# Placing 56 modulation tiles in another way in a one-core diffusion-layer kernel, with a new order of the first attention head and another split of the second half-step's norm

## The chip, the cores and the metric

The kernel runs on one core of one Trainium2 chip. The time is that of the whole program on the device, in microseconds (us). A core has a matrix engine (TensorE, PE in the profile, with its weight loads listed apart as PEld), a vector engine (VectorE, DVE), a scalar engine (ScalarE, ACT), GpSimd (POOL) and a sequencer that mostly issues DMAs (SyncE, SP). [...]

## The reference, cut to what matters

One layer of a diffusion trunk on 512 latent and 128 context tokens, 1024 channels wide: a half-step of a gated feed-forward network, token mixing (differential attention beside a bidirectional chunkwise mLSTM), and a second half-step. Nine modulation vectors per token kind scale, shift and gate the three stages:

```python
def adaln(cvec, w, b):
    m = jax.nn.silu(cvec) @ w + b          # w_ada: 1024 x 9*1024
    return m.reshape(cvec.shape[0], N_MOD, D_MODEL)

def layer(x, mods, l, p, ctx):
    m = [mods[:, j][:, None, :] for j in range(N_MOD)]
    g = p['g_norm'][l]
    hh = rmsnorm(x, g[0]) * (1 + m[1]) + m[0]
    x = x + 0.5 * m[2] * swiglu(hh, p['ffn1_w1'][l], p['ffn1_w3'][l], p['ffn1_w2'][l])
    hh = rmsnorm(x, g[1]) * (1 + m[4]) + m[3]
    y, ctx_out = token_mixer(hh, p, l, ctx)
    x = x + m[5] * y
    hh = rmsnorm(x, g[2]) * (1 + m[7]) + m[6]
    x = x + 0.5 * m[8] * swiglu(hh, p['ffn2_w1'][l], p['ffn2_w3'][l], p['ffn2_w2'][l])
    return x, ctx_out
```

The modulation is computed twice, with `c` for the latent tokens and with `c_ctx` for the context tokens. In the mixer the attention has 8 heads of two 64-wide query and key halves (each normed, and rotated by position), whose two softmaxes are subtracted; the mLSTM has 4 heads and walks over chunks of 128 tokens in both directions. The two branches go through `w_br_d` and `w_br_m`, are gated, added, and projected by `w_out`.

## The kernel before, in words

**Arithmetic.** Everything is fp32. For TensorE each operand is split into a high part in a shorter format and a low remainder, and a product is three matmuls: high by high, high by low, low by high (`mm3`). A split of a weight is a copy on ScalarE (`wH`, `ww`, `wB`) and a subtraction on VectorE (`wL`). The 640 token columns are worked on in two halves of 320.

**Stages, in order.** (1) Startup and the first two modulation vectors, on TensorE. (2) The first half-step's up products: 18 steps of `products`. (3) Its down products: three groups of the hidden width (`PLAIN_GROUPS`), four steps each, of which eight (20 to 27) call `modulation`. (4) The second norm, the first queries' and keys' projection in token groups (`tok_group` with `w_q`, then `w_k`). (5) Eight attention heads, one loop, with five query blocks `qi` each; between the steps `fill` hands out units of the projections that come later (values, gates, mLSTM queries and keys), so that TensorE has work beside the softmax. (6) Four mLSTM heads of ten chunk cells each (`Memory`), again with `fill` units between the cells. (7) The branch projections `w_brd` and `w_brm`, eight granules of four columns' products, then `w_out` and the third norm (`normed`). (8) The second half-step, which ends with the output.

**The modulation tiles.** 56 tiles of 128 channels remain after the startup, each for one of seven modulation vectors. `Columns` hands them out in order. `place(n, csil, load, ahead)` sets how many come next, from which conditioning rows (`csil`, silu of `c` and of `c_ctx`, spread over all partitions), how a raw tile of `w_ada` is loaded, and how many loads run ahead. `tile` runs two `tensor_tensor_reduce` passes over 128 x 1024 on VectorE, one for each token kind, and then fetches the next. When the eight tiles of a vector are done, its bias is added, and a callback makes what the later stages use: vector 0 (numbered among these seven) gives the first half-step's gate, 1 and 2 the second norm's shift and scale, 3 the mixer's gate, 4 and 5 the third norm's, 6 the last gate.

**Where they stand.** `modulation(i, at)` is called in each of the first half-step's steps, twice (`at` 0 and 1). In steps 2 to 17 it runs one tile for `at` 1, and one more for `at` 0 where `i % 8 == 4`: 18 tiles. In the down products' steps 20 to 27 it runs one tile for `at` 0 and two for `at` 1: 24 tiles. Their raw tiles, rows and scratch lie in the buffers tagged `BL`, `BH` and `CH`, which the last down group's weights (`wB`) use as well. The last 14 stand in the attention loop, in heads 0 to 5; their raw tiles take buffers of the ring `raw` (two buffers), through which all projection weights pass, and their rows lie in `q3` and `k3`, which the fourth pair of queries and keys takes later.

**Head 0.** `Head.pack` copies a head's queries (`qpk`) and keys (`kpk`, `kp2`) into split parts; `queries` and `keys` turn them on TensorE. For head 0 `pack` and `queries` stand in the setup behind both token groups, where `qk_norm_rope` has normed and rotated the queries and then the keys on VectorE.

**The third norm.** `normed` takes one half of the columns. Half 1 consists of 192 latent and 128 context columns (`SEGS`), which have modulation vectors of their own, so each of its eight channel blocks takes two segments of three instructions: scale and divide by the norm on VectorE (`x<-x,scale,ry`), add the shift on ScalarE into the high part `hm`, and subtract on VectorE for the low part. `x` itself is left without its shift; sixteen `activate` instructions (eight blocks by two segments) add it behind the first products, before `operand_sums` adds up blocks of `x` for the second half-step's operands (`S`).

## Time and profile before

Three runs took 1905.3, 1905.95 and 1911.75 us (median 1905.95). The profiled execution has a span of 1909.6 us from its first to its last instruction, that is 3.65 us above the median and within the runs. Its mean granted TensorE clock is 0.982 of full speed.

The stages, each as a stretch of the profiled span (busy time in us; the borders are rounded):

| stretch, us | stage | PE busy | DVE busy | ACT busy | granted clock |
|---|---|---|---|---|---|
| 0 to 60 | startup, first norm | 39.48 | 44.84 | 33.34 | 0.94 |
| 60 to 320 | up products, half-step 1 | 254.15 | 223.70 | 130.39 | 1.00 |
| 320 to 500 | down products, half-step 1 | 167.81 | 126.42 | 35.10 | 0.96 |
| 500 to 575 | second norm, first queries and keys | 64.83 | 57.47 | 38.74 | 0.93 |
| 575 to 1126 | attention heads | 538.14 | 340.07 | 244.45 | 0.99 |
| 1126 to 1290 | mLSTM cells | 158.71 | 98.20 | 95.57 | 0.98 |
| 1290 to 1411 | branch projections | 120.32 | 57.81 | 46.96 | 1.00 |
| 1411 to 1500 | `w_out`, third norm | 88.75 | 63.02 | 47.96 | 1.00 |
| 1500 to 1909 | half-step 2 | 390.34 | 294.62 | 171.73 | 0.98 |

How to read what follows. A line of the timeline has the start, the duration, the engine, the source line, the operation, and what it writes (left of the arrow) and reads; in brackets stands how long its engine had been idle before it, and whose end released it. A line of the groups has busy time and mean duration in ns, then the idle time before and its main releaser. The granted clock is the share of full speed that the chip gave TensorE. The source lines of small helpers (L39, L42, L52, L55) are shared by many operations, so the names of the tiles tell which one it is.

### The profile page before, as it was taken

Reading aid. Unit: us, or ns where it says so; the run is one execution under the profiler, and the core shown is the slowest. Engines: PE = TensorE matmul, PEld = TensorE weight load, DVE = VectorE, ACT = ScalarE, POOL = GpSimd, SP = SyncE. Lnnn points to the kernel's source line nnn. Section 1 sums busy time; section 2 is a strip of 40 time slices with the busy share of each in tenths; the row PEclk is TensorE's granted clock in tenths of the full one; section 3 lists DMA queues with packets and bytes.
Section 4 is the critical chain, followed back from the end, with each engine's and each line's share of the span. In section 5 each row is a group of like instructions: output and inputs, shape, how many; then the busy total and the mean of one; then the engine's idle time right before and its main releaser. Section 6 shows DMA issues by size and latency. Waiting matters only on the chain.

```text
span 1909.6 us, 30786 instructions
## 1 busy us (share of the span) xinstructions
PE 1822.5 (95%) x12658; PEld 1782.0 (93%) x12658; DVE 1306.1 (68%) x2209; ACT 844.2 (44%) x1447; POOL 42.4 (2%) x69
## 2 busy tenths in 40 slices
PE   6999999998989999999999989999999899999989
PEld 4999999998888999999999989899999899999989
DVE  7889986578686566775765536664457778886575
ACT  5644443212353353453544446655234655554232
POOL 1000001010000000000000000000000000000000
PEclk9999999998999999999999999999999899999999
DMA  8354558965314223223221342445442344447952
GB/s 322 117 180 166 174 182 303 339 218 168 139 45 163 98 75 120 79 92 104 70 102 60 107 165 93 141 149 211 163 141 83 127 144 176 174 174 268 346 188 94
DMA packets 127150, 298.77 MB, mean 156 GB/s; under 512 B 9441, under 2 KB 90593, under 8 KB 114337
## 3 DMA queue, kind: packets, MB, share of 16 engines
q1 hardware_dynamic: 115762, 248.58, 37.4%
q0 software_dynamic: 11248, 48.24, 7.0%
q8 instruction: 99, 1.62, 0.4%
q14 instruction: 41, 0.34, 0.1%
HBM read 233.15 MB, written 63.63 MB: 155 GB/s over the span
## 4 chain that ended last, share of the span: by engine, by line
PE 78%; DVE 9%; DMA 8%; issue 3%; ACT 2%; SPq 0%; POOL 0%; DVEq 0%; ACTq 0%; POOLq 0%
PE ps_f L52 35%; PE ps_p L52 21%; PE ps_t L52 11%; PE ps_o L52 2%; PE sc L52 2%; DMA ada<-in_w_ada_c 2%; PE ps_n L52 2%; DVE ww L39 1%; PE ps_wT L55 1%; DMA ada<-csil_dram 1%; PE ps_u L52 1%; PE ps_qkT L55 1%; DMA raw<-in_w2a 1%; DVE ada L671 1%; DVE junk L671 1%
## 5 line engine op out<-in xcount | busy, mean ns | idle before, releaser
L52 PE MATMUL ps_f<-S,ww 128*128 128x320 f32 x1992 | 321.3, 310 | 14.2 <-ACT ww L267 6.9
L52 PEld LDWEIGHTS ps_f<-S,ww 128*128 128x128 f32 x1992 | 299.9, 189 | 16.7 <-DVE ww L39 9.5
L52 PE MATMUL ps_p<-hH,wH 128*128 128x320 f32 x864 | 275.3, 319 | 3.1 <-ACT aT L1313 2.5
L52 PE MATMUL ps_p<-hH,wL 128*128 128x320 f32 x864 | 268.2, 310 | 0.0
L52 PE MATMUL ps_p<-hL,wH 128*128 128x320 f32 x864 | 268.2, 310 | 0.0
L52 PE MATMUL ps_f<-hm,ww 128*128 128x320 f32 x1248 | 198.7, 311 | 9.8 <-ACT ww L267 5.6
L52 PEld LDWEIGHTS ps_f<-hm,ww 128*128 128x128 f32 x1248 | 188.2, 190 | 11.1 <-ACT ww L267 5.9
L52 PE MATMUL ps_t<-wH,hH 128*128 128x256 f32 x640 | 186.6, 292 | 0.9 <-DVE x L42 0.9
L52 PE MATMUL ps_t<-wH,hL 128*128 128x256 f32 x640 | 182.7, 285 | 0.0
L52 PE MATMUL ps_t<-wL,hH 128*128 128x256 f32 x640 | 182.3, 285 | 0.0
L39 DVE TENSOR_TENSOR ww<-raw,ww 128x2048 fp32r<-128x2048 f32 (+1 forms) x62 | 138.7, 2237 | 51.9 <-ACT ww L267 29.7
L52 PEld LDWEIGHTS ps_p<-hH,wH 128*128 128x128 f32 x864 | 163.8, 190 | 4.3 <-ACT aT L1313 2.7
L52 PEld LDWEIGHTS ps_p<-hL,wH 128*128 128x128 f32 x864 | 163.8, 190 | 0.5
L52 PEld LDWEIGHTS ps_p<-hH,wL 128*128 128x128 f32 x864 | 163.4, 189 | 0.0
L52 PE MATMUL ps_f<-hm,wB 128*128 128x320 f32 x1008 | 161.5, 309 | 0.0
L52 PEld LDWEIGHTS ps_f<-hm,wB 128*128 128x128 f32 x1008 | 151.3, 188 | 0.0
L39 DVE TENSOR_TENSOR wL<-raw,wH 128x2048 fp32r<-128x2048 f32 x49 | 112.1, 2288 | 38.1 <-ACT wH L123 37.9
L123 ACT ACTIVATE wH<-raw 128x2048 fp32r<-128x2048 f32 x49 | 93.6, 1911 | 99.0 <-PE ps_p L52 89.5
L52 PEld LDWEIGHTS ps_t<-wH,hH 128*128 128x128 f32 x640 | 124.1, 194 | 1.9 <-ACT hH L201 1.7
L39 DVE TENSOR_TENSOR raw<-raw 128x1024 f32<-128x1024 f32 (+1 forms) x144 | 124.1, 865 | 1.7
L267 ACT ACTIVATE ww<-raw 128x2048 fp32r<-128x2048 f32 x48 | 91.7, 1911 | 74.7 <-PE ps_f L52 47.3
L52 PEld LDWEIGHTS ps_t<-wH,hL 128*128 128x128 f32 x640 | 123.9, 194 | 0.5 <-DVE hL L42 0.5
(294 smaller groups left out, 3251.5 us busy)
## 6 DMA issues: line engine op xcount, KB each, us to landing
g_dram<-g SPq DMA_DIRECT2D x44, 640.0 KB, 5.0
ada<-in_w_ada_c POOLq DMA_DIRECT2D x24, 512.0 KB, 4.9
raw<-in_w1b SPq DMA_DIRECT2D x11, 1024.0 KB, 4.8
raw<-in_w3b SPq DMA_DIRECT2D x11, 1024.0 KB, 4.8
raw<-in_w1a SPq DMA_DIRECT2D x10, 1024.0 KB, 4.8
raw<-in_w3a SPq DMA_DIRECT2D x10, 1024.0 KB, 7.0
hm<-g_dram POOLq DMA_DIRECT2D x8, 1280.0 KB, 10.2
raw_a<-in_w_ada_c POOLq DMA_DIRECT2D x18, 512.0 KB, 5.3
```

The costliest lines, as they stand in the source:

```text
L39: return eng.tensor_tensor(out=out, in0=in0, in1=in1, op=op)
L52: tc.keep_in_program_order(nc.tensor.matmul(*args, **kw))
L55: tc.keep_in_program_order(nc.tensor.transpose(*args, **kw))
L123: act(h, raw, AF.Copy)
L267: act(t[0], flat, AF.Copy)
L671: vec.tensor_tensor_reduce(out=junk, in0=raw, in1=self.csil[:, v, :], op0=ALU.mult, op1=ALU.add, scale=1.0, scalar=0.0, accum_out=mod[:, c ...
```

## The change

- The up products take 8 tiles (in even steps, `at` 1) instead of 18, the down products 16 (one for each call) instead of 24.
- The attention takes 9, in the blocks 0 to 2 of heads 1 to 3, instead of 14. Their raw tile and scratch lie in the buffers `q2` and `k2`, no longer in the ring.
- The remaining 23 stand behind the attention: ten in the mLSTM cells, two in the last mLSTM head's end, the others between the units of the branch projections. They load through the ring again. Their conditioning rows are loaded anew, 1 MB on SP's queue, into a pool of their own that is opened at the attention's end. A load is issued only where `fetch` says so, two units or cells ahead of its tile.
- Head 0's queries are packed directly behind the queries' token group, and its keys later, behind `queries`. Its square scratch (`sq`) lies in the buffer of `qT`.
- The third norm divides by the norm for a block's whole half at once, adds scale and shift by ScalarE in place, segment by segment, copies the high part whole on ScalarE and subtracts whole on VectorE. `x` then holds its shift, and the sixteen later `activate` instructions go.

```diff
-        def fetch(self):
-            while len(self.next) < min(self.ahead, self.n):
+        def fetch(self, ahead=0):
+            while len(self.next) < min(ahead or self.ahead, self.n):
...
-        columns.place(18, csil, load_columns)
+        columns.place(8, csil, load_columns)
...
-                if 2 <= i < 18 and (at or i % 8 == 4):
+                if 2 <= i < 18 and at and i % 2 == 0:
                     columns.tile(hs.at_vec)
...
-                    columns.place(24, csil, load_columns)
+                    columns.place(16, csil, load_columns)
                 columns.tile(hs.at_vec)
-                if at:
-                    columns.tile(hs.at_vec)
...
-        sq = ap.tile([128, 5, 256], F32, tag="pk", name="sq", bufs=2)
+        if pr:
+            sq = ap.tile([128, 5, 256], F32, tag="pk", name="sq", bufs=2)
+        else:
+            sq = ap.tile([128, 5, 256], F32, tag="qT", name="sq")
...
         def pack(self):
-
+            self.pack_q()
+            self.pack_k()
...
             self.turn_features(self.qpk, self.qT, False, lambda o, i: act(o, i, AF.Copy))
+            if self.hd:
+                self.low_keys()
...
     tok_group(psum, [(w_q, i, e_q) for i in (2, 3, 4)], lambda k: None)
+    heads = [Head(hd) for hd in range(8)]
+    heads[0].pack_q()
     tok_group(psum, [(w_k, i, e_k) for i in (2, 3, 4)], lambda k: None)
...
-        heads[0].pack()
         heads[0].queries()
+        heads[0].pack_k()
+        heads[0].low_keys()
...
     def load_columns(src):
-        t = rawp.tile([128, 2048], F32, tag="raw", name="raw_a")
-        dma(t[:, :D], src)
-        return t[:, :D], t[:, D : D + D // 2].bitcast(BF16)
+        t = pair("q", 2, "raw_a").rearrange("p a t -> p (a t)")[:, :D]
+        junk = pair("k", 2, "junk").rearrange("p a t -> p (a t)")[:, : D // 2].bitcast(BF16)
+        dma(t, src)
+        return t, junk
...
-    columns.place(14, csil, load_columns, 1)
+    columns.place(9, csil, load_columns, 1)
...
-            if hd < 6 and qi in (1, 3) or (hd, qi) in ((2, 2), (4, 2)):
+            if hd in (1, 2, 3) and qi < 3:
                 columns.tile()
...
+    cs = ExitStack()
+    cs_p = cs.enter_context(tc.tile_pool(name="csil", bufs=1, side="right"))
+    csil = cs_p.tile([128, 2, D], F32, name="csil")
+    for v in range(2):
+        nc.sync.dma_start(out=csil[:, v, :], in_=csil_dram[v].partition_broadcast(128))
...
+    columns.place(23, csil, load_columns, 0)
...
             fill.slot(0)
+            if len(box_ml) % 4 == 0:
+                columns.fetch(1)
+            elif len(box_ml) % 4 == 2:
+                columns.tile()
+            box_ml.append(0)
         m.stats()
...
         mem[3].finish(i)
+        columns.fetch((i + 1) % 2)
+        if i % 2:
+            columns.tile()
...
+    def drain_beside_columns():
+        n = 0
+        while fill.q:
+            columns.fetch((n + 1) % 2)
+            fill.one()
+            if n % 2 and columns.n:
+                columns.tile()
+            n += 1
...
+            xs = x[d][:, half(hf)]
+            h, lo = hs.hh(d, hf)
+            tt(vec, xs, xs, rs, ALU.mult)
             for s0, s1, j in SEGS[hf]:
-                xs = x[d][:, s0:s1]
-                h, lo = (t[:, s0 - c0 : s1 - c0] for t in hs.hh(d, hf))
-                sh = shift[:, d, j : j + 1]
-                stt(xs, xs, scale[:, 2, d, j : j + 1], rs[:, s0 - c0 : s1 - c0], ALU.mult, ALU.mult)
-                act(h, xs, AF.Identity, bias=sh)
-                ins = stt(lo, xs, sh, h.bitcast(F32), ALU.add, ALU.subtract)
+                v = x[d][:, s0:s1]
+                act(v, v, AF.Identity, bias=shift[:, d, j : j + 1], scale=scale[:, 2, d, j : j + 1])
+            act(h, xs, AF.Copy)
+            ins = tt(vec, lo, xs, h.bitcast(F32), ALU.subtract)
...
-    for d in range(KT):
-        for s0, s1, j in ((0, NS, 0), (NS, T, 1)):
-            xs = x[d][:, s0:s1]
-            act(xs, xs, AF.Identity, bias=m_of(6)[:, d, j : j + 1])
     summed = hs.operand_sums(lambda r: x_pairs[r])
```

More of the change, by code (lines that the diff above doesn't have):

```diff
@@ L1125, in gate_cols, with qk_norm_rope @@
             )
-    def qk_norm_rope(raw, tab):
+    def qk_norm_rope(raw, tab, pr):
         A, B, g = tab
-        sq = ap.tile([128, 5, 256], F32, tag="pk", name="sq", bufs=2)
+        if pr:
+            sq = ap.tile([128, 5, 256], F32, tag="pk", name="sq", bufs=2)
+        else:
+            sq = ap.tile([128, 5, 256], F32, tag="qT", name="sq")
         act(sq, raw, AF.Square)
@@ L1158, in evac @@
                 if i == 4:
-                    qk_norm_rope(t, tabs[0])
+                    qk_norm_rope(t, tabs[0], pr)
             return evac
@@ L1171, in evac @@
                 if i == 4:
-                    qk_norm_rope(t, tabs[1])
+                    qk_norm_rope(t, tabs[1], pr)
                     nc.sync.dma_start(out=a["new_k"][:, pr * 256 : (pr + 1) * 256], in_=t[:, 4, :])
@@ L1199, in pack, with pack_q @@
         def pack(self):
+            self.pack_q()
+            self.pack_k()
+        def pack_q(self):
             hs = slice(self.h * 128, (self.h + 1) * 128)
             qv = q_tok[self.pr][:, :, hs].rearrange("p t (c d) -> p t c d", c=2)
-            kv = self.kv = k_tok[self.pr][:, :, hs].rearrange("p t (c d) -> p t c d", c=2)
             self.qpk = ap.tile([128, 5, 4, 64], F32R, tag="pk", name="qpk", bufs=2)
@@ L1206, in pack, with pack_k @@
             tt(vec, self.qpk[:, :, 1:3, :], qv, self.qpk[:, :, 0::3, :].bitcast(F32), ALU.subtract)
+        def pack_k(self):
+            hs = slice(self.h * 128, (self.h + 1) * 128)
+            kv = self.kv = k_tok[self.pr][:, :, hs].rearrange("p t (c d) -> p t c d", c=2)
             self.kpk = ap.tile([128, 5, 4, 64], F32R, tag="pk", name="kpk", bufs=2)
@@ L1226, in queries, with low_keys @@
             self.turn_features(self.qpk, self.qT, False, lambda o, i: act(o, i, AF.Copy))
+            if self.hd:
+                self.low_keys()
+            ck = load(ap, [128, 2, 256], a["cache_kd"][:, self.hd], tag="asq", name="ck")
+            act(self.kH[:, :, 512:768], ck, AF.Copy)
+            tt(vec, self.kL[:, :, 512:768], ck, self.kH[:, :, 512:768].bitcast(F32), ALU.subtract)
+        def low_keys(self):
             self.kp2 = ap.tile([128, 5, 4, 64], F32R, tag="pk", name="kp2", bufs=2)
@@ L1229, in queries @@
                 self.at_vec = tt(vec, self.kp2[:, :, i::2, :], self.kv, self.kpk[:, :, i::2, :].bitcast(F32), ALU.subtract)
-            ck = load(ap, [128, 2, 256], a["cache_kd"][:, self.hd], tag="asq", name="ck")
-            act(self.kH[:, :, 512:768], ck, AF.Copy)
-            tt(vec, self.kL[:, :, 512:768], ck, self.kH[:, :, 512:768].bitcast(F32), ALU.subtract)
         def keys(self, part):
@@ L1383, in gate_evac @@
         return f
-    heads = [Head(hd) for hd in range(8)]
     with tc.tile_pool(name="gates", bufs=1) as gt:
@@ L1518, in tile_trunk, with load_columns @@
     att.close()
+    cs = ExitStack()
[3 more added lines that the diff above has]
+        nc.sync.dma_start(out=csil[:, v, :], in_=csil_dram[v].partition_broadcast(128))
+    def load_columns(src):
+        t = rawp.tile([128, 2048], F32, tag="raw", name="raw_a")
+        dma(t[:, :D], src)
+        return t[:, :D], t[:, D : D + D // 2].bitcast(BF16)
+    columns.place(23, csil, load_columns, 0)
     ml = ExitStack()
@@ L1668, in attended @@
         aHL.append(split_part(attended.raw[:, k % 3], t))
+    box_ml = []
     mem = [Memory(h) for h in range(4)]
@@ L1731, in tile_trunk @@
         tt(vec, zL[:, k], raw[:, k % 3], zH[:, k].bitcast(F32), ALU.subtract)
-    fill.drain()
+    def drain_beside_columns():
[6 more added lines that the diff above has]
+            n += 1
+    drain_beside_columns()
     ml.close()
@@ L1760, in tile_trunk @@
             nc.sync.dma_start(out=x_pairs[g], in_=x_dram[:, 2 * g : 2 * g + 2, :])
-        fill.drain()
+        drain_beside_columns()
+    cs.close()
     fp = out.enter_context(tc.tile_pool(name="out", bufs=1))
@@ L1805, in normed @@
         rs = st[hf].rstd(psum)
-        c0 = hf * HALF
         shift = m_of(6)
         for d in range(KT):
+            xs = x[d][:, half(hf)]
+            h, lo = hs.hh(d, hf)
+            tt(vec, xs, xs, rs, ALU.mult)
             for s0, s1, j in SEGS[hf]:
-                xs = x[d][:, s0:s1]
-                h, lo = (t[:, s0 - c0 : s1 - c0] for t in hs.hh(d, hf))
-                sh = shift[:, d, j : j + 1]
-                stt(xs, xs, scale[:, 2, d, j : j + 1], rs[:, s0 - c0 : s1 - c0], ALU.mult, ALU.mult)
-                act(h, xs, AF.Identity, bias=sh)
-                ins = stt(lo, xs, sh, h.bitcast(F32), ALU.add, ALU.subtract)
+                v = x[d][:, s0:s1]
+                act(v, v, AF.Identity, bias=shift[:, d, j : j + 1], scale=scale[:, 2, d, j : j + 1])
+            act(h, xs, AF.Copy)
+            ins = tt(vec, lo, xs, h.bitcast(F32), ALU.subtract)
         return ins.ins
```

## The prediction

> **What bounds the kernel now.** I read the engine shares first, then the chain that ended last, then the span in stretches of 20 us, and last the stalls of TensorE one by one in its timeline.
>
> ```profile
> span 1909.6 us, 30786 instructions
> PE 1822.5 (95%) x12658; PEld 1782.0 (93%) x12658; DVE 1306.1 (68%) x2209; ACT 844.2 (44%) x1447; POOL 42.4 (2%) x69
> PE 78%; DVE 9%; DMA 8%; issue 3%; ACT 2%; SPq 0%; POOL 0%; DVEq 0%; ACTq 0%; POOLq 0%
> ...
> 60.00:80.00 20.00, 20.00 (x140) 20.00 (x139) 17.81 (x28) 15.42 (x24) 0.00 (x0) 1.00 0.23 81
> 440.00:460.00 20.00, 14.17 (x97) 13.91 (x95) 17.79 (x33) 1.57 (x3) 2.65 (x5) 0.91 0.54 176
> 460.00:480.00 20.00, 16.96 (x93) 16.57 (x94) 13.92 (x22) 8.18 (x10) 0.00 (x0) 0.75 0.49 170
> 600.00:620.00 20.00, 19.07 (x117) 18.89 (x118) 13.40 (x17) 9.22 (x14) 0.00 (x0) 0.84 0.56 206
> ```
>
> TensorE is busy for all but 87 us of the span and carries 78% of the chain. No matmul is added or taken away, so the change can win only what TensorE idles, plus what it loses at a lower granted clock after idling. The columns of the stretches are length, busy time and count of PE, PEld, DVE, ACT, POOL, then granted clock. An undisturbed stretch holds 140 matmuls, 0.143 us each; the two from 440 to 480 hold 97 and 93, at clocks 0.91 and 0.75. These are TensorE's stalls that the change can touch, with what released it in brackets:
>
> ```profile
> 136.77 1.73 PE L52 MATMUL ps_f<-S,ww 128*128 128x320 f32 x10 [2.56 <-DVE ww L39]
> 239.06 1.15 PE L52 MATMUL ps_f<-S,ww 128*128 128x320 f32 x6 [2.57 <-DVE ww L39]
> 462.16 0.90 PE L52 MATMUL ps_f<-S,wB 128*128 128x320 f32 x2 [7.99 <-ACT wB L285]
> 555.63 1.50 PE L55 MATMUL ps_qkT<-identr,qpk 128*128 128x128 f32 x10 [5.93 <-DVE qpk L39]
> 600.93 1.51 PE L55 MATMUL ps_wT<-ident,p 128*128 128x128 f32 x6 [4.33 <-DVE p L42]
> 742.16 0.87 PE L55 MATMUL ps_wT<-ident,p 128*128 128x128 f32 x6 [1.66 <-DVE p L42]
> 879.22 1.03 PE L55 MATMUL ps_wT<-ident,p 128*128 128x128 f32 x5 [1.91 <-DVE p L42]
> 1515.73 0.90 PE L52 MATMUL ps_f<-S,ww 128*128 128x320 f32 x2 [6.91 <-ACT ww L267]
> 1518.05 2.24 PE L52 MATMUL ps_f<-S,ww 128*128 128x320 f32 x7 [1.42 <-DVE ww L39]
> ```
>
> **The change part by part.** A modulation tile is two passes on VectorE, one DMA of 512 KB, and nothing on TensorE:
>
> ```profile
> L671 DVE CUSTOM_DVE_ANT_0 ada<-ada 128x1024 bf16<-128x1024 f32 x48 | 58.6, 1221 | 17.8 <-DMA ada<-in_w_ada_c 12.0 <-DMA ada<-csil_dram 5.5
> L671 DVE DVE_READ_ACCUMULATOR2_ANT mod<- 128x1 f32 x112 | 9.3, 83 | 0.0
> ```
>
> So a tile costs about 2 x 1.22 = 2.45 us of VectorE; the accumulator reads overlap nearly all of their 0.083 us.
>
> *Up products, 18 tiles to 8.* The stalls at 136.77 and 239.06 wait for a weight's low part on VectorE, which is full there. They fall where the old rule puts two tiles into one step (steps 4 and 12, `i % 8 == 4`). The new rule puts one there: 2.45 us less VectorE ahead of a wait of 2.56. Gain 5.1 (bounds 0 and 5.1). Ten loads leave POOL's queue, where nothing waits for them.
>
> *Down products, 24 tiles to 16.* The conditioning rows and raw tiles lie in the buffers tagged B and C that the last down group's weights need:
>
> ```profile
> 351.97 1.23 DVE L671 CUSTOM_DVE_ANT_0 ada<-ada 128x1024 bf16<-128x1024 f32 x1 [5.46 <-DMA ada<-csil_dram]
> 461.05 1.06 ACT L285 ACTIVATE wB<-raw 128x1024 fp32r<-128x1024 f32 x1 [2.22 <-DVE mod L671]
> 461.52 1.22 DVE L671 CUSTOM_DVE_ANT_0 ada<-ada 128x1024 bf16<-128x1024 f32 x1
> ```
>
> ScalarE's split of `wB` waits for the tiles, and the last pass starts at 461.52. The second of the 48 passes gets its rows at 351.97; from there on the 24 tiles take some 4.6 us each (110 us by 24), their loads waiting for the two raw buffers. Sixteen at that pace end near 352 + 16 x 4.6 = 426, before TensorE has got to the step that the last one is tied to (about 438). `wB` can then be split some 10 us before TensorE wants it at 454. The two stretches lack 280 - 190 = 90 matmuls: gain 90 x 0.143 = 12.9 us, taken as 12.7 (bounds 6, if the 6 us of other stalls there stay, and 12.9).
>
> *Head 0's queries first.* At 555.63 TensorE waits for `qpk`:
>
> ```profile
> 545.05 1.22 DVE L39 TENSOR_TENSOR q_tok<-q_tok,sw 128x1024 f32<-128x1024 f32 x1
> 552.35 0.72 ACT L1205 ACTIVATE qpk<-q_tok 128x640 fp32r<-128x640 f32 x1
> 577.57 1.74 DVE L1262 TENSOR_REDUCE mx<-sc 128x2 f32<-128x1536 f32 x1
> ```
>
> The queries are ready at 546.3, but their packing stands behind the keys' rope and starts at 552.35. Moved ahead of the keys it ends near 548, while TensorE is still busy (until 549.7). So 5.93 us of idle go, with some 1.6 us of half clock. But what is late next is VectorE: keys' rope, `kp2`, the gates' scans, then head 0's first softmax, whose `mx` runs at 577.57 although its scores are there 3 us earlier. That row of work starts only about 1 us sooner, while TensorE comes 6 us sooner and must wait for the score bank. Bounds: 1.0 (VectorE decides) and 7.5 (the softmax slips in between). I take 4.5. `sq` moves to the buffer of `qT`, which is empty then: nothing.
>
> *Nine tiles in heads 1 to 3, in buffers of their own.* The old ones go through the weights' raw ring, and VectorE stands still in front of them:
>
> ```profile
> 594.61 1.22 DVE L671 CUSTOM_DVE_ANT_0 raw_a<-raw_a,csil 128x1024 bf16<-128x1024 f32 x1 [6.25 <-DMA csil<-csil_dram]
> 877.00 1.23 DVE L671 CUSTOM_DVE_ANT_0 raw_a<-raw_a,csil 128x1024 bf16<-128x1024 f32 x1 [1.51 <-DMA raw_a<-in_w_ada_c]
> ```
>
> The tile at 594.61 waits 6.25 us for its rows, and head 0's softmax, whose `p` TensorE awaits at 600.93, stands behind it. Head 0 has no tile any more: 4.33 us go, and with them the low clock that follows (0.84 over 20 us is 3.2; 2.8 of it on busy time): 7.1. The stalls at 742 and 879 have a tile, waiting for its DMA, ahead of `p`. A load now starts when the tile before is done, some 13 us ahead, so its two passes start without a wait and no longer hold `p` up. Gain 1.66 + 1.91 = 3.6. Bounds together 5 and 11.
>
> *Second half-step's norm.*
>
> ```profile
> 1475.83 4.57 DVE L42 SCALAR_TENSOR_TENSOR x<-x,scale,ry 128x192 f32<-128x192 f32 x15
> 1476.28 4.93 ACT L1814 ACTIVATE hm<-x,mod 128x192 fp32r<-128x192 f32 x15 [2.07 <-DVE x L42]
> 1489.05 0.83 DVE L39 TENSOR_TENSOR x<-x 128x640 f32<-128x640 f32 x1 [1.61 <-ACT x L1846]
> 1490.86 1.56 DVE L39 TENSOR_TENSOR x<-x 128x640 f32<-128x640 f32 x2 [0.99 <-ACT x L1846]
> L1846 ACT ACTIVATE x<-x,mod 128x512 f32<-128x512 f32 x8 | 5.7, 716 | 0.0
> L39 DVE TENSOR_TENSOR nacc<-nacc,nsq 128x320 f32<-128x320 f32 x36 | 17.6, 490 | 16.4 <-ACT nsq L181 15.0
> ```
>
> VectorE's second half falls from 32 pieces at 0.305 us (4.57 by 15), 9.8 us, to 16 whole ones at 0.49 or less, 7.8 at most. ScalarE gets eight copies there (about 0.45 each: 3.6) and drops the shifts behind (16, of which the eight long ones are 5.7 us). The norm is now paced by ScalarE, about 8 x (2 x 0.33 + 0.4) = 8.5 us, so it ends near 1485 as before. What goes is the wait of the operand sums for the shifts, 1.61 + 0.99 = 2.6 us, and sums can start in VectorE's gaps before 1485. From 1491 VectorE works without a pause up to the weights that TensorE awaits at 1515.73 and 1518.05 (8.3 us idle). Gain 5 (bounds 1.5 and 9, the latter with the clock that follows).
>
> *23 tiles behind the attention.* New here: two loads of the conditioning rows (1 MB) on SP's queue, then ten tiles in the mLSTM cells and 13 in the projections, loaded through the raw ring.
>
> ```profile
> 1137.34 0.83 DVE L39 TENSOR_TENSOR P<-P,mask 128x640 f32<-128x640 f32 x1 [7.69 <-DMA P<-nm_dram]
> 1137.61 0.71 PE L52 MATMUL ps_st<-mqT,mkT 128*128 128x128 f32 x4 [1.42 <-ACT stage L1381]
> 1240.00:1260.00 20.00, 20.00 (x123) 18.36 (x121) 14.88 (x48) 12.27 (x36) 0.00 (x0) 1.00 0.50 160
> DVE C L42 <- PE ps_u L52: 23.3, 15, 4.0
> L39 DVE TENSOR_TENSOR wL<-raw,wH 128x2048 fp32r<-128x2048 f32 x49 | 112.1, 2288 | 38.1 <-ACT wH L123 37.9
> raw_a<-in_w_ada_c SPq DMA_DIRECT2D x14, 512.0 KB, 3.9
> raw<-in_w_brm SPq DMA_DIRECT2D x4, 1024.0 KB, 6.9
> 1339.73 1.92 ACT L123 ACTIVATE wH<-raw 128x2048 fp32r<-128x2048 f32 x1 [12.22 <-PE ps_p L52]
> ```
>
> The rows are issued ahead of `va` and `P`, for which VectorE and ScalarE already stand still and TensorE begins to wait at 1136. In head 0 VectorE stood 6.25 us for the same rows (above). I price the delay at 4.5 (bounds 0 and 7). In the cells VectorE is busy 15 of 20 us and waits 23.3 us for TensorE in all; a pass of 1.22 us can hold up an update of `C`, for which the next cell but one has about 2 us of slack: ten tiles, 0.3 us each, 3 (bounds 0 and 24.5). In the projections ScalarE waits 12.22 us with the next weight already there, so the ring has slack: 1 for the 13 (bounds 0 and 40, below).
>
> **Sum:** -5.1 - 12.7 - 4.5 - 7.1 - 3.6 - 5.0 + 4.5 + 3 + 1 = -29.5. The span of 1909.6 becomes 1880; it is 3.65 above the median of 1905.95, and lies within the runs (1905.3 to 1911.75), so I forecast 1905.95 - 29.5 = **1876 us**.
>
> [...]
>
> **Rivals.** (1) *The cells pay for the tiles*: each of the ten exposes one pass or more (1.22 to 2.45) and the rows cost 7. That is 12 to 24 instead of 3 and 2.5 more: 1888 to 1900. For it: VectorE is in order and the cells are a recurrence; against it: its 5 idle us in 20. (2) *Head 0 and the last norm give nothing*, as VectorE's row of work decides both: 1.0 + 1.5 for 9.5: 1883. (3) *The change doesn't free the last down group*: `wB` then waits for its own weight's DMA or for a tile tied late; 6 us less: 1882. (4) *Slower: the ring starves the projections.* It has two buffers, and a weight (load 6.9, split 1.9 + 2.3) and two tiles (3.9 + 2.45 each) must pass in the 14.1 us of a granule. Were they to follow each other on one buffer, 11.1 + 12.7 = 23.8 us a granule, 9.7 more, eight times: 1954. It outweighs the rest from 29.5 / 8 = 3.7 us per granule. Against it: the two buffers offer 28 us for 24.
>
> **How the numbers follow.** Forecast (1868 to 1884) 0.55; rival 2 or 3 alone 0.15 (within or close to it); both, or rival 1: 0.20; rival 4: 0.05; better than 1868 0.05. The best bounds together give -45, the worst of the gains with the dear cells about -10. The range is 1861 to 1895. A measurement of this kernel can tell about 0.5% (9.5 us) from no change: faster 0.83, same 0.10, slower 0.07.
>
> **What would show it.** Right: no stall over 1 us near 137, 239, 462, 600, 742 and 879; the stretches 440 to 480 at 138 to 140 matmuls each; the first score bank as the next stall behind 550; under 5 us idle ahead of the second half-step's first sums. Wrong: `PE <- DVE C` or `num` in the cells, ACT `wH` waiting for DMA in the projections, or `wB` still behind `mod`.

## The result, and the profile after

The changed kernel takes 1893.48 us (median of four runs, 1888.11 to 1896.81), the kernel before 1905.62 us beside it: a ratio of 0.9924 with a 95% interval of 0.9902 to 0.9947. In later runs it was 1894.09 and 0.9934 (0.9918 to 0.9951). So it is faster by 12 to 13 us, and not by the 29.5 that lead to the forecast of 1876. The time lies in the range of 1861 to 1895, near its upper end.

The page of the changed kernel begins like this (span, engine shares, chain of waits by engine):

```profile
span 1890.2 us, 30782 instructions
PE 1816.4 (96%) x12658; PEld 1778.2 (94%) x12658; DVE 1299.5 (69%) x2193; ACT 847.0 (45%) x1447; POOL 32.9 (2%) x51
PE 79%; DVE 9%; DMA 7%; ACT 3%; issue 2%; SPq 0%; DVEq 0%; ACTq 0%
```

The matmuls are the same 12658; TensorE's idle time in the span fell from 87 us to 74. The stretches that answer to those shown of before, and one more (length, busy time and count of PE, PEld, DVE, ACT, POOL, granted clock, DMA share, GB/s):

```profile
440.00:460.00 20.00, 20.00 (x138) 20.00 (x137) 9.87 (x18) 5.58 (x9) 0.00 (x0) 1.00 0.23 79
460.00:480.00 20.00, 19.14 (x129) 18.59 (x128) 14.60 (x35) 7.11 (x14) 0.00 (x0) 1.00 0.20 68
600.00:620.00 20.00, 18.49 (x141) 18.20 (x140) 16.02 (x31) 6.98 (x16) 0.00 (x0) 1.00 0.39 132
1320.00:1340.00 20.00, 15.33 (x90) 15.10 (x89) 12.54 (x19) 3.82 (x2) 0.00 (x0) 0.83 0.78 290
```

From 440 to 480 the row now has 138 and 129 matmuls instead of 97 and 93 (the second stretch already holds the next stage's beginning). The last row shows a new loss: the changed kernel has 90 matmuls from 1320 to 1340, where before had 138:

```profile
1320.00:1340.00 20.00, 20.00 (x138) 20.00 (x138) 6.60 (x12) 3.74 (x5) 0.00 (x0) 1.00 0.37 137
```

TensorE's stalls in the changed kernel's timeline show the same:

```profile
348.82 3.02 PE L52 MATMUL ps_f<-hm,ww 128*128 128x320 f32 x10 [2.14 <-DVE ww L39]
536.09 1.28 PE L55 MATMUL ps_qkT<-identr,kpk 128*128 128x128 f32 x10 [1.72 <-ACT kpk L1216]
562.53 0.87 PE L55 MATMUL ps_wT<-ident,p 128*128 128x128 f32 x6 [3.25 <-DVE p L42]
636.88 0.87 PE L55 MATMUL ps_wT<-ident,p 128*128 128x128 f32 x6 [1.73 <-DVE p L42]
1111.88 1.20 PE L52 MATMUL ps_n<-va,P 128*128 128x258 f32 x2 [4.60 <-DVE P L39]
1333.87 0.60 PE L52 MATMUL ps_p<-hH,wH 128*128 128x320 f32 x1 [4.67 <-DVE y L39]
1495.49 0.71 PE L52 MATMUL ps_f<-S,ww 128*128 128x320 f32 x2 [2.74 <-ACT ww L267]
1497.82 2.50 PE L52 MATMUL ps_f<-S,ww 128*128 128x320 f32 x8 [1.62 <-DVE ww L39]
```

The stalls at 137, 239, 462, 601, 742 and 879 are gone. New ones stand at 562.53 and 636.88, ahead of `p`, and, longer, at 1111.88 and 1333.87. To see what each stage won or lost, take a product that both kernels have at its border, and subtract its start. Here are the borders in the timeline of before (the second norm, the attention's end, a product in the first and one in the last mLSTM cells, the third norm), and then the same products in that of the changed kernel:

```profile
506.07 0.81 PE L52 MATMUL ps_ss<-nacc,ones 128*128 128x320 f32 x2 [3.45 <-DVE nacc L39]
1126.67 0.41 PE L52 MATMUL ps_p<-hH,wH 128*128 128x320 f32 x1 [2.47 <-ACT aT L1313]
1156.41 0.60 PE L52 MATMUL ps_n<-va,P 128*128 128x258 f32 x2
1287.97 0.60 PE L52 MATMUL ps_n<-va,P 128*128 128x258 f32 x2
1470.10 0.70 PE L52 MATMUL ps_ss<-nacc,ones 128*128 128x320 f32 x2
```

```profile
484.83 0.91 PE L52 MATMUL ps_ss<-nacc,ones 128*128 128x320 f32 x2 [3.46 <-DVE nacc L39]
1095.12 0.41 PE L52 MATMUL ps_p<-hH,wH 128*128 128x320 f32 x1 [2.47 <-ACT aT L1324]
1127.31 0.59 PE L52 MATMUL ps_n<-va,P 128*128 128x258 f32 x2
1261.84 0.59 PE L52 MATMUL ps_n<-va,P 128*128 128x258 f32 x2
1451.62 0.70 PE L52 MATMUL ps_ss<-nacc,ones 128*128 128x320 f32 x2
```

The lag is -21.24 at the second norm, -31.55 at the attention's end, -29.10 in the first mLSTM cells, -26.13 in the last, -18.48 at the third norm and -19.4 at the end of the span. Its steps, beside the forecast's terms and the same sums for a second profile of the changed kernel (after_again, whose span is 1892.1):

| stage | forecast, us | changed kernel | after_again |
|---|---|---|---|
| startup and half-step 1 | -17.8 | -21.2 | -19.3 |
| head 0 and attention | -15.2 | -10.3 | -8.2 |
| conditioning rows, first cells | +4.5 | +2.5 | +1.1 |
| other cells | +3.0 | +3.0 | +2.1 |
| projections | +1.0 | +7.7 | +7.6 |
| third norm, half-step 2 | -5.0 | -0.9 | -0.8 |
| sum | -29.5 | -19.4 | -17.5 |

### The profile page after: what moved, and what is told of

It is laid out like the page before. It is cut to its first block, busy times and chain, and to the rows that moved or that the text cites. A ratio compares the mean times of both kernels' runs of the same rounds, so it can differ in the third digit from the quotient of the medians.

```text
span 1890.2 us, 30782 instructions
## 1 busy us (share of the span) xinstructions
PE 1816.4 (96%) x12658; PEld 1778.2 (94%) x12658; DVE 1299.5 (69%) x2193; ACT 847.0 (45%) x1447; POOL 32.9 (2%) x51
## 4 chain that ended last, share of the span: by engine, by line
PE 79%; DVE 9%; DMA 7%; ACT 3%; issue 2%; SPq 0%; DVEq 0%; ACTq 0%
PE ps_f L52 41%; PE ps_p L52 17%; PE ps_t L52 11%; DMA raw_a<-in_w_ada_c 3%; PE sc L52 2%; PE ps_o L52 2%; DMA ada<-csil_dram 1%; PE ps_n L52 1%; DVE junk L671 1%; PE ps_wT L55 1%; DMA P<-nm_dram 1%; PE ps_qkT L55 1%; DVE raw_a L671 1%; PE ps_u L52 1%; DVE wL L39 1%
## 5 line engine op out<-in xcount | busy, mean ns | idle before, releaser
L52 PEld LDWEIGHTS ps_f<-hm,ww 128*128 128x128 f32 x1248 | 190.4, 192 | 10.3 <-ACT ww L267 5.9
L52 PEld LDWEIGHTS ps_t<-wL,hH 128*128 128x128 f32 x640 | 123.7, 193 | 0.3 <-issue 0.2
```

The lines of the kernel that those rows point to most:

```text
L52: tc.keep_in_program_order(nc.tensor.matmul(*args, **kw))
```

## The experiments

All times stand beside runs of the kernel before on the same chip. The spread of one kernel's runs is some 5 to 10 us, so a difference under 3 us is read from the traces, not from the times.

### The two kernels again

before_again is the kernel before, after_again the changed kernel, both without an edit.

> The kernel before, unchanged, to see what differs between two profiled executions of one kernel. The profiled execution of before took 1911.75 us, 6 us above the other three (1905.3 to 1906). Theory A: it held a stall that the usual execution has not (first candidate: the 6.25 us for the conditioning rows in head 0, whose removal I priced at 7.1); then this profile has a span near 1903.5, and one or two of the stalls at 137, 239, 359, 462, 556, 601, 742, 879 are missing or over 2 us shorter. Theory B: the 6 us lie spread over many places, all those stalls are there within 0.5 us, and the forecast's terms stand. Ratio to before 1.000 within 0.002.

Measured: 1908.38 us, ratio 1.0009 (0.9995 to 1.0023), span 1908.9. The profile has all those stalls: 2.56, 2.55, 2.27, 6.37, 5.92, 3.62, 1.58 and 1.96 us where the first had 2.56, 2.57, 2.70, 7.99, 5.93, 4.33, 1.66 and 1.91. Theory B holds in the main: all the stalls are there, though not within its 0.5 us. They differ by up to 0.7, the one of 7.99 by 1.6. The trace on which the forecast rests is no odd one, though both profiled executions of before (1911.75 and 1910.65 us) are longer than the medians beside them by 2 to 6 us.

> The changed kernel again, more rounds. If the first profile was an ordinary execution: span 1890 to 1893, a ratio to before of 0.990 to 0.992. If it was a good one: ratio 0.992 to 0.994, and the new profile shows where executions differ. Own_ym3 against this run is 6 to 10 us if the projections' 7.7 us are what it wins.

Measured: 1894.09 us, ratio 0.9934, span 1892.1. The span fits the first case of the expectation and the ratio the second, so the first profile was at most some 2 us better than an ordinary one. The two traces of the changed kernel differ by 2 us in half-step 1 and by 2 us in the attention, with the same large stalls in the same places.

### The hand-over from w_brd to w_brm

A drain is the loop that runs the units still left in `fill`, with a tile behind every second one: the first drain ends the `w_brd` products, the second does the `w_brm` products. Between the two a new PSUM pool is opened. What happened there, before the stall at 1333.87, is seen on SP, ScalarE and VectorE of the changed kernel:

```profile
1305.46 16.50 SPq L74 DMA_DIRECT2D raw_a<-in_w_ada_c  x4
1324.32 3.96 SPq L74 DMA_DIRECT2D raw<-in_w_brm  x2
1329.09 1.91 ACT L123 ACTIVATE wH<-raw 128x2048 fp32r<-128x2048 f32 x1 [17.93 <-PE ps_p L52]
1331.03 2.29 DVE L39 TENSOR_TENSOR wL<-raw,wH 128x2048 fp32r<-128x2048 f32 x1 [2.31 <-ACT wH L123]
1333.24 0.48 DVE L39 TENSOR_TENSOR y<-ps_p,sig 128x320 f32<-128x320 f32 x1
```

Four tiles' loads occupy the ring for 16.5 us; the first `w_brm` weight, which the program has behind them, is issued at 1324.32 and split by 1333.3. In before it was issued at 1320.98, more than 30 us ahead of its use. The stall is put down to `y`, and rightly: the `y` at 1333.24 is the last of sixteen, and with it the last evacuation of the old PSUM pool. TensorE's last `w_brd` product had ended at 1329.2, but this `y` stands on VectorE behind `wL`, the split of the late weight, for which VectorE idles 2.31 us until `wH` is done. So the late weight holds TensorE up by way of the last `y`.

brm_early queues the weight ahead of the last two tiles (the first drain ends when four granules are left):

```diff
+    for g in range(4):
+        fill.granule(a["w_brm"][g], lambda g=g: feat_units(psum, m_evac(g), zHL))
-    drain_beside_columns()
+    drain_beside_columns(4)
```

> The changed kernel with the four w_brm granules queued ahead of the first drain, so that the first of their weights is loaded ahead of the drain's last two tiles. Theory: the 7.7 us lost between 1300 and 1340 come from the raw ring; the four tiles of the first drain hold both buffers, and the first w_brm weight is issued only at 1324.3, split until 1333. Then the stall of 4.67 us (released at 1333.87) and the low clock behind it go: 5 to 8 us faster than the changed kernel (about 1886 to 1888.5; ratio to before 0.989 to 0.991). Rival: VectorE's own work (ten passes of 1.22 us among the evacuations) makes the loss; then the stall stays or moves, and the time is within 2 us of the changed kernel's 1893.5.

Measured: 1892.24 us, ratio 0.9924. The weight was split by 1325.9, and the stall stayed:

```profile
1329.59 1.23 DVE L671 CUSTOM_DVE_ANT_0 raw_a<-raw_a,csil 128x1024 bf16<-128x1024 f32 x1 [1.00 <-DMA raw_a<-in_w_ada_c]
1332.29 0.48 DVE L39 TENSOR_TENSOR y<-ps_p,sig 128x320 f32<-128x320 f32 x1
1332.92 0.61 PE L52 MATMUL ps_p<-hH,wH 128*128 128x320 f32 x1 [5.63 <-DVE y L39]
```

The rival came true in a narrower form. The next product needs a bank of the new PSUM pool, so it waits for the last `y`; here this `y` stood on VectorE behind a tile that had waited for its load, and no longer behind `wL`.

tail_clear leaves no tile to the last `w_brd` granule; early_clear does both (`clear` is 8 in the first drain and 0 in the second):

```diff
-            columns.fetch((n + 1) % 2)
+            room = columns.n > clear
+            columns.fetch((n + 1) % 2 if room else 0)
...
-            if n % 2 and columns.n:
+            if n % 2 and room:
                 columns.tile()
```

> The changed kernel without tiles beside the last w_brd granule: the first drain has three tiles instead of five, the second eight instead of six. In brm_early the weight was ready at 1325.8 and TensorE still waited 5.63 us, for the last evacuations `y` of the old PSUM pool, which stood on VectorE behind two tiles and their DMA. Theory (the tiles hold back both the last `y` and the next weight): the stall behind the last w_brd product falls from 4.67 to under 2 us, the loss between 1300 and 1340 from 7.7 to 1 to 3 us: 5 to 7 us faster than the changed kernel (1886.5 to 1888.5). Rival (the raw ring alone: the first w_brm weight still stands behind the w_brd granules' program): a stall of 3 us or more stays there.

> Both: the w_brm granules queued early and no tiles beside the last w_brd granule. If both causes count (weight and `y`), only this run brings the stall to that of before (0.67 us): 6 to 8 us faster than the changed kernel (1885.5 to 1887.5), and up to 3 us faster than tail_clear. If `y` alone counts, it equals tail_clear within 1 us.

Measured: 1893.15 us (0.9927) and 1895.70 us (0.9949). Both expectations failed. VectorE of early_clear shows why:

```profile
1336.64 1.23 DVE L671 CUSTOM_DVE_ANT_0 raw_a<-raw_a,csil 128x1024 bf16<-128x1024 f32 x1 [6.47 <-DMA raw_a<-in_w_ada_c]
1339.06 0.48 DVE L39 TENSOR_TENSOR y<-ps_p,sig 128x320 f32<-128x320 f32 x1
```

This tile belongs to the second drain in the program. The framework that orders each engine's instructions has put it ahead of the last `y`, where it found VectorE free; on the chip it waits 6.47 us for its load, and TensorE 8.74 us behind it. In tail_clear the tile waited 4.26 and TensorE 6.54.

tied holds the tiles back by an order, clear_tied adds tail_clear, and clear_tied_rows the late rows (below):

```diff
-            tt(vec, y1[g][:, mt, half(hf)], p, t, ALU.mult)
+            box["y"] = tt(vec, y1[g][:, mt, half(hf)], p, t, ALU.mult)
...
-                tt(vec, yL[:, d, cs], t, yH[:, d, cs].bitcast(F32), ALU.subtract)
+                box["y"] = tt(vec, yL[:, d, cs], t, yH[:, d, cs].bitcast(F32), ALU.subtract)
...
-                columns.tile()
+                columns.tile(box["y"])
```

> The changed kernel with each of the two drains' tiles tied behind the evacuation of its own unit (`y`, or `yL` behind `ym`), nothing else. In tail_clear and early_clear the last `y` still stood on VectorE behind a tile that waited 4.26 and 6.47 us for its DMA; it had been pulled ahead of its unit. Theory (a tile pulled forward blocks the last evacuation, and the new PSUM pool waits for it): no tile stands ahead of the last `y` any more, but the first w_brm weight is still loaded late (1324), so 1 to 4 us of the 7.7 come back: 1889.5 to 1892.5. Rival (raw ring alone): within 1 us of 1893.5.

> tied, and no tiles beside the last w_brd granule, so that the first w_brm weight is split by about 1325 (as in tail_clear) and the last `y` is free. Theory: the stall falls from 4.67 to under 1.5 us, and the loss between the cells' end and the third norm from 7.7 to under 2.5 us: 5 to 7 us faster than the changed kernel (1886.5 to 1888.5). Rival (VectorE's amount of work counts, not its order): the tiles now stand ahead of `wL` of the next weights, a stall of over 3 us appears in the w_brm granules, and the time is within 2 us of 1893.5.

> clear_tied and the late conditioning rows of rows_late together. rows_late's lag against the changed kernel went from +0.88 us at the attention's end to -2.33 in the second cells: 3.2 us. If both gains add: 8 to 10 us faster than the changed kernel (1883.5 to 1885.5; ratio to before 0.987 to 0.989). If the time won at the cells' start is lost again in the cells (a tile that waits for the rows), 1886.5 to 1888.5.

Measured: 1912.48 us (1.0026), 1909.08 (1.0012) and 1903.98 (0.9996): by their medians 19, 16 and 10 us slower than the changed kernel, a large miss. In tied:

```profile
1321.33 9.34 SPq L74 DMA_DIRECT2D raw_a<-in_w_ada_c  x3
1337.36 0.33 SPq L74 DMA_DIRECT2D raw<-in_w_brm  x1
1348.39 0.64 PE L52 MATMUL ps_p<-hH,wH 128*128 128x320 f32 x1 [10.48 <-ACT wH L123]
```

The last `y` is free now, but a tile that may not run keeps its half of the ring until it runs, so the weight is issued 13 us later than in the changed kernel. clear_tied has 0.68 us at the hand-over and waits for `wH` of 3.29 us at 1318 and 4.96 at 1402 instead. From the last cells to the third norm tied takes 209.23 us, 27.1 more than before. This is the forecast's rival 4, the starved ring, at about a third of the 77.6 us that it was priced at.

The next runs take the tiles out of the ring. own_buffers gives them buffers of their own (in the first drain those of `so` and `C0`, which are empty by then); own_tied ties them too; own_tied_rows adds the late rows:

```diff
+    def own_ml():
+        t = mp.tile([128, 2, T], F32, tag="so", name="raw_a").rearrange("p a t -> p (a t)")[:, :D]
+        junk = mp.tile([128, 2, 258], F32, tag="C0", name="junk", bufs=2)
...
+        junk_gp = gp.tile([128, D], BF16, name="junk")
+        box["own"] = lambda: (gp.tile([128, D], F32, tag="raw_a", name="raw_a"), junk_gp)
...
-            t = gp.tile([128, HALF], F32, tag="ym", name="ym", bufs=3)
+            t = gp.tile([128, HALF], F32, tag="ym", name="ym")
```

> The changed kernel with the drains' tiles in buffers of their own (first drain: that of `so` and `C0`, which are empty by then; second: one raw tile in the gate pool, for which `ym` goes from three buffers to one); the ring holds weights alone. No tie. If the ring is the cause: no wait for `wH` or `wL` in the projections, the stall of 4.67 falls under 1.5 us, 6 to 7 us faster than the changed kernel (1886.5 to 1887.5). If the tile ahead of the last `y` is the cause: the stall stays at 3 to 6 us with the weight ready long before, and the time is within 2 us of 1893.5.

> own_buffers, and each tile of the drains tied behind its own unit's evacuation. Where tied starved the ring (10.48 us ahead of `wH`), here no weight can wait for a tile. Theory (both causes): no stall over 1.5 us between 1290 and 1420, the loss of 7.7 falls to 1 to 2: 1886 to 1888. Rival (VectorE's 27 us of passes are too much beside the evacuations): stalls of 1 to 3 us at several units, and 1890 or more.

> own_tied and the late rows of rows_late. If both gains stand beside each other: 1882.5 to 1885.5, ratio to before 0.987 to 0.989, and clear of the changed kernel's 0.9924. If one of them is lost again behind: 1886 to 1890.

Measured: 1895.82 us (0.9948), 1902.28 (0.9979) and 1898.93 (0.9964), all longer than expected. The hand-over of own_buffers costs 0.68 us, as before the change, but the single `ym` buffer makes two new stalls at the end of the projections:

```profile
1393.28 0.63 PE L52 MATMUL ps_p<-hH,wH 128*128 128x320 f32 x1 [3.59 <-ACT hH L1810]
1399.43 0.64 PE L52 MATMUL ps_p<-hH,wH 128*128 128x320 f32 x1 [4.72 <-ACT hH L1810]
```

So the time told nothing of the ring. Tying costs here too: from the last cells to the third norm own_tied takes 199.20 us and own_buffers 193.40, though no weight waits for a tile in either. own_ym3 gives `ym` its three buffers back and lays the scratch into the last pair of `x`, which is then loaded behind the drain; own_ym3_rows adds the late rows:

```diff
-        junk_gp = gp.tile([128, D], BF16, name="junk")
+        junk_gp = x_pairs[3][:, 0, : D // 2].bitcast(BF16)
...
-        for g in range(4):
+        for g in range(3):
             nc.sync.dma_start(out=x_pairs[g], in_=x_dram[:, 2 * g : 2 * g + 2, :])
...
+        nc.sync.dma_start(out=x_pairs[3], in_=x_dram[:, 6:8, :])
```

> own_buffers with `ym` in three buffers again (the passes' scratch now lies in the last pair of `x`, which is loaded behind the second drain). Theory (the 7.7 us of the projections come from the ring): no stall over 1 us between 1300 and 1440, and 5 to 7 us faster than the changed kernel (1886.5 to 1888.5, ratio to before 0.989 to 0.990). Rival: what the ring gives is taken by VectorE elsewhere in the projections (waits for `yH` or `wL`): 1891.5 or more.

> own_ym3 and the late rows of rows_late (3.2 us by the traces' lag up to the second cells). If both add: 1883 to 1886, ratio to before 0.987 to 0.989, below the changed kernel's 0.9924. If the rows' gain is lost: 1886.5 to 1889.

Measured: 1881.74 us, ratio 0.9876 (0.9856 to 0.9897), and 1882.39 us, 0.9881 (0.9862 to 0.9899). Both are shorter than expected, and shorter than both kernels of this study. From own_ym3, the hand-over, its stretch, the cells' end and the third norm:

```profile
1328.66 0.38 PE L52 MATMUL ps_p<-hH,wH 128*128 128x320 f32 x1 [0.68 <-DVE y L39]
1262.09 0.60 PE L52 MATMUL ps_n<-va,P 128*128 128x258 f32 x2
1444.21 0.70 PE L52 MATMUL ps_ss<-nacc,ones 128*128 128x320 f32 x2
```

```profile
1320.00:1340.00 20.00, 19.32 (x132) 19.09 (x131) 13.06 (x19) 4.80 (x4) 0.00 (x0) 1.00 0.88 328
```

Between the last two products lie 182.12 us, in before 1470.10 - 1287.97 = 182.13, in the changed kernel 1451.62 - 1261.84 = 189.78. The whole 7.7 us are back. The same tiles still run on VectorE, untied, some of them ahead of evacuations; with loads that need no ring they wait less (at most 2.96 us in the first drain), and no weight waits for them. The edit ends both ways to the stall at once: the weight is early, and the second drain's first tile runs at 1335.31, behind the hand-over. Each way alone is enough for a stall (4.67 us behind the late weight's split, 5.63 behind a tile in brm_early), and the runs do not divide the 7.7 us between them. The times put the gain at some 12 us instead of 7.7, which is within the spread of both.

### The conditioning rows

rows_late moves the two loads behind the first mLSTM head's own:

```diff
     mem[0].load()
     mem[0].load_c()
+    for v in range(2):
+        nc.sync.dma_start(out=csil[:, v, :], in_=csil_dram[v].partition_broadcast(128))
```

> The changed kernel with the two loads of conditioning rows issued behind the first mLSTM head's loads of `va`, `P` and `C`. Theory: the stall of 4.60 us ahead of the first `va` by `P` product (before: 1.42 + 0.96 + 0.38) comes from the rows' 1 MB ahead of them in SP's queue; then it falls to about 1 to 2 us and the first cells start 2 to 3.5 us sooner (1890 to 1891.5). Rival: the first tile of the cells, which waits for the same rows, now stands on VectorE ahead of the cells' work; then the stall moves into the first cells and the time stays within 1 us of 1893.5.

Measured: 1891.29 us, ratio 0.9924. The stall in the first cells and the stretch around it, first in rows_late, then the stretch in the changed kernel:

```profile
1109.64 0.70 PE L52 MATMUL ps_n<-va,P 128*128 128x258 f32 x2 [1.49 <-DVE P L39]
```

```profile
1110.00:1120.00 10.00, 8.25 (x37) 6.44 (x36) 10.00 (x23) 5.90 (x16) 0.00 (x0) 1.00 1.08 376
```

```profile
1110.00:1120.00 10.00, 8.12 (x26) 6.71 (x27) 6.30 (x16) 7.65 (x23) 0.00 (x0) 0.66 1.06 377
```

The wait of 4.60 us became 1.49, and the clock of the stretch 1.00 instead of 0.66 (in the ten microseconds before, 0.97 instead of 1.00). Other short waits take part of it back: TensorE is busy for 8.25 of the ten microseconds, against 8.12. From the attention's end to the cell that starts at 1127.31 in the changed kernel rows_late takes 28.99 us instead of 32.19, so the rows' place costs 3.2 us there. In the end it is not clear in the times: 2.2 us less here, and 0.65 more in own_ym3_rows than in own_ym3, whose spans differ by 1.7 the other way.

### Head 0's order, and the attention's tiles

head0_old undoes the new order (`pack` and `queries` behind both token groups, `sq` in its old buffer).

> The changed kernel with head 0's old order (queries and keys packed together behind both token groups). Forecast of the prediction: 4.5 us slower than the changed kernel (1898). What the two traces show instead: up to head 0's first value product the change gained only 0.64 us more than before that stage, since VectorE's softmax chain (the reduce of mx, the scans, p) decides; by that theory 0 to 1.5 us slower (1893.5 to 1895).

Measured: 1892.76 us, 0.9934. The traces set out alike (the norm's sums 0.06 us apart) and stand 1.6 us apart at the attention's end, in favour of the new order. That is less than the 2 us by which the two traces of the changed kernel differ in this stage, and the time is no longer than the changed kernel's, so a gain is not shown. More telling is what is left in head0_old, VectorE and TensorE:

```profile
572.90 1.22 DVE L671 CUSTOM_DVE_ANT_0 junk<-raw_a,csil 128x1024 bf16<-128x1024 f32 x1 [6.01 <-DMA raw_a<-in_w_ada_c]
577.07 1.51 PE L55 MATMUL ps_wT<-ident,p 128*128 128x128 f32 x6 [4.16 <-DVE p L42]
```

This is head 0, which has no tile in the program: the stall that had 4.33 us before is there all the same, with 4.16. The tiles of heads 1 to 3 are pulled forward, like those of the second drain. In the changed kernel all nine run in heads 0 and 1, and with the new order the first comes just behind `p` instead of ahead of it:

```profile
574.94 1.23 DVE L671 CUSTOM_DVE_ANT_0 junk<-raw_a,csil 128x1024 bf16<-128x1024 f32 x1 [2.68 <-DMA gm_dram<-stage]
634.20 1.22 DVE L671 CUSTOM_DVE_ANT_0 junk<-raw_a,csil 128x1024 bf16<-128x1024 f32 x1
```

tiles_pinned ties each tile behind its block's `p` (`self.at_p = stt(p0[...], ...)`, then `columns.tile(H.at_p)`).

> The changed kernel with each of the attention's nine tiles tied behind the `p` of its own block. In the changed kernel all nine run between 575 and 635, in heads 0 and 1, ahead of where the program has them. Theory: their pull forward makes the stalls of head 1 (1.10 at 606.08, 1.73 at 636.88 and the low clock behind); 4.3 us were lost there against before. Tied, the tiles spread over heads 1 to 3 and the loss falls to under 1 us: 3 to 4 us faster (1889.5 to 1890.5). Rival: a tile costs the softmax as much wherever it stands; then the stalls move to heads 2 and 3, and the time is within 1.5 us of 1893.5.

Measured: 1893.42 us, 0.9939. The tiles spread, and the traces show both theories at work: against the changed kernel 4.7 us are won up to the end of head 1 (from a lag of 1.3 to one of 6.0) and 4.2 lost again in the heads behind, where new waits appear:

```profile
810.60 0.85 PE L55 MATMUL ps_wT<-ident,p 128*128 128x128 f32 x6 [1.59 <-DVE p L42]
```

The rival's number came out: in these two placements the tiles cost the softmax about as much. In the changed kernel no low clock stands behind the two stalls of head 1: it was 1.00 in each stretch of 20 us from 600 to 660.

### The third norm

norm_old is the changed kernel with the old pieces and the shifts behind (the diff above, reversed), own_norm_old the same edit on own_ym3_rows.

> The changed kernel with the third norm in its old pieces. Forecast of the prediction: 5 us slower than the changed kernel (1898.5). What the two traces show: the half-step behind the norm loses 2.4 us ahead of the first sums and wins 4.2 us in the weights' waits at 1495 and 1498, 0.9 us in the end; by that theory 0 to 2 us slower (1893.5 to 1895.5).

> own_ym3_rows with the third norm in its old pieces. By the prediction's term: 5 us slower than own_ym3_rows (1887.4). By the traces of norm_old (2.4 us lost at 1466 to 1476 by ScalarE's pace, 4.2 won at 1495): 0 to 2 us slower (1882 to 1884.5).

Measured: 1892.66 us (0.9922) and 1884.42 (0.9884). The first is 0.8 us shorter than the changed kernel, the second 2.0 longer than own_ym3_rows, both within the spread. By the traces, from the norm's sums to the end of the span, the new norm is worth 0.8 us in the first pair and 3.0 in the second. The same ten microseconds, in the changed kernel and then in norm_old, and the first wait for a weight in norm_old:

```profile
1466.00:1476.00 10.00, 8.65 (x53) 7.64 (x53) 8.63 (x15) 7.69 (x14) 0.00 (x0) 1.00 0.00 0
```

```profile
1466.00:1476.00 10.00, 10.00 (x70) 10.00 (x70) 7.30 (x9) 8.94 (x17) 0.00 (x0) 1.00 0.01 2
```

```profile
1494.88 0.90 PE L52 MATMUL ps_f<-S,ww 128*128 128x320 f32 x2 [6.90 <-ACT ww L267]
```

The new norm takes this wait from 6.90 to 2.74 us, and pays for it ahead: TensorE runs 53 matmuls where it could run 70 (17 x 0.143 = 2.4 us), as `hm` now comes from ScalarE at its pace (in the changed kernel its last copy ends at 1469.56, in norm_old its last piece at 1461.28).

## Why the prediction was right or wrong

*Right in sign and in the first half.* The up products' two stalls went, the last down tile ends at 431.2 (forecast 426), `wB` is ready in time, and the stretches from 440 to 480 are full up to the next stage. The term of 17.8 us measured 19.3 to 21.2, of which the first trace owes 0.9 to the startup (the first up products start at 50.62 instead of 51.55), where the change does nothing. A smaller stall shrank with it (2.70 us at 359.16 before, 2.14 at 348.82 now), and the second profile shows that 2 us of it vary between executions.

*Head 0's queries: mis-sized.* Priced 4.5 (bounds 1.0 and 7.5), worth 1.6 at most. The bound "VectorE decides" was the nearer one: the stall of 5.93 became 1.72, and one of 3.25 ahead of `p` came behind it.

*Nine tiles in heads 1 to 3: the step failed.* "Head 0 has no tile any more" was read from the program; the instructions' order on the engine is another. The stall of 4.33 went because of the new order, not for want of a tile, and the tiles pulled forward cost head 1 part of it again: the lag shrinks from 28.4 us at its first turned queries (632.52 and 604.09) to 24.7 at those of head 2 (705.53 and 680.87). The two steps together gave 8.2 to 10.3 instead of 15.2.

*The rows and the cells: right, somewhat overpriced.* Together 7.5 forecast, 5.4 measured in one trace and 3.2 in the other. Rival 1 (12 to 24 us for the cells) did not come, though the measured time lies in its bracket of 1888 to 1900.

*The projections: the step failed.* "The ring has slack: 1 for the 13" was read from ScalarE's wait for TensorE inside the w_brm granules. The slack was missing at one place, between two drains, where the next weight is not prefetched ahead of the tiles, and where TensorE waits for one last evacuation that stands on VectorE behind what the ring has made late. A sign that the forecast had named for this came: ScalarE's `wH` waits 7.89 us for a weight's DMA at 1309.24. Rival 4 named the mechanism and priced it for all eight granules (77.6 us ahead of the gains); it struck once, for 7.7. With the tiles out of the ring the loss is gone (182.12 us against 182.13), so the ring is shown as the cause; how much goes by the weight and how much by the tiles' loads is not. It accounts for 6.7 of the 10.1 us between the forecast and the pair of traces.

*The third norm: mis-sized.* Priced 5.0 (bounds 1.5 and 9), worth 0.8 to 3.0. The step that failed is "it ends near 1485 as before". The forecast gave ScalarE 8.5 us for the second half; it took 11.7 (1457.89 to 1469.56), with other work and a table load of 1.28 us in between. The last low part ends 19.4 us behind the norm's sums, where before had 15.3, so TensorE had its `hm` later, and part of what the weights' waits gave was paid for there.

*The range: luck.* Its upper end does not follow from the bounds. The lowest gains add up to 13.5 us, and the dear cells with the dear rows and 1 for the projections cost 20 to 32, which would be slower than before and not 10 us faster. The time lies inside the range by 1.5 us, while three terms (the attention, the projections, the third norm) missed.

*What the runs leave open.* The spans of before and of the changed kernel, two profiles each, stand 17 to 19 us apart, the medians of timed runs 12 to 13. So of the 17 us between the forecast and the medians, 10 have a place in the table and some 7 have none. The sum was read from a trace of an execution of 1911.75 us and taken off a median of 1905.95. Over the runs of before on record the time goes with the mean granted clock: 0.975 to 0.979 in the four longest (1912.19 to 1914.81 us), 0.985 to 0.987 in the four shortest (1899.42 to 1901.35). Which stalls make the difference no trace tells, as the other executions have none.

*The clock behind a stall.* The rows' new stall came with a low clock: 4.60 us of idling, and a granted clock of 0.66 over the ten microseconds from 1110. That is 3.4 us of clock (10 x 0.34), of which 0.9 lie in the stall itself (the clock is about 0.50 from 1110.0 to 1116.9, and the stall ends at 1111.88), so 2.5 us are lost. The forecast's 4.5 for the rows has no term for this. A low clock also came behind shorter stalls: behind the one of 1.72 us at 536.09 it was 0.50 from 538 to 540, behind the one of 3.25 us at 562.53 the stretch from 560 to 580 has 0.91, and in before, behind the one of 1.91 us at 879.22, it was 0.50 from 880 to 882. Behind the stall of 1.73 us at 636.88 it stayed at 1.00.

```profile
560.00:580.00 20.00, 17.47 (x117) 17.25 (x117) 12.96 (x20) 7.59 (x14) 0.00 (x0) 0.91 0.60 207
```

## What to carry to other kernels

Filler work that shares a buffer ring with weights must be judged at the places where the prefetch chain breaks (between two queues of work, at a change of pools), not by the ring's average slack. Where a scheduler orders the engines, the program's place of an instruction says little: ask for the order on the engine before you credit a stage with losing it. And a filler that waits for a DMA needs its buffer long before: tying it late without a buffer of its own made the time longer by 19 us, giving it a buffer made it shorter by 12 (7.7 by the traces).

## What was not expected of the hardware

Two stalls, of 4.60 and 4.67 us, cost TensorE about half as much again each. The stretches around them (1110 to 1120 and 1320 to 1340) show clocks of 0.66 and 0.83, that is 3.4 us of clock each (10 x 0.34 and 20 x 0.17). The low clock set in before the stall was over (0.52 already from 1110 to 1111, where the first ends at 1111.88, and 0.50 from 1332 to the end of the second at 1333.87), so about 1 us of it cost nothing, and 2.4 to 2.5 us were lost on top of each stall. In rows_late, where the first is 1.49 us, the clock in the same stretch is 1.00, and 0.97 in the ten microseconds before. The length of a short stall did not tell in the changed kernel: the one of 1.72 us at 536.09 was followed by a clock of 0.50, the one of 1.73 us at 636.88 by 1.00.
